# Sums of weight quarters for seven SwiGLU pairs and for the last product: made by GpSimd in the buffers that the products read, instead of ahead and through DRAM

## The chip, the cores and the metric

One core of one Trainium2 chip runs the whole block. The metric is device time in microseconds of one launch; a kernel's time is the median of its runs. The engines are named as the profile names them: PE is TensorE, PEld its weight loads, DVE is VectorE, ACT is ScalarE, POOL is GpSimd and SP is SyncE, which only issues DMAs. A q behind a name is the engine's queue of DMA issues.

## The reference, cut to what matters

Everything is fp32: 512 positions, width 1024, SwiGLU width 2816.

```python
h = rmsnorm(x, norm1_g)
z_glu, z_rx, z_rg, z_ga, z_gb = split(h @ w_in + b_in)     # 2048, 1280, 1280, 1024, 1024
u = z_glu[..., :1024] * sigmoid(z_glu[..., 1024:])
u = silu(layernorm(causal_depthwise_conv(u, 31 taps)))
y_a = u @ conv_w_out + conv_b_out
y_b = (rg_lru(causal_depthwise_conv(z_rx, 4 taps)) * gelu(z_rg)) @ lru_w_out
x = x + (sigmoid(z_ga) * y_a + sigmoid(z_gb) * y_b) @ w_mix_out
h = rmsnorm(x, norm2_g)
x = x + (silu(h @ ffn_w1) * (h @ ffn_w3)) @ ffn_w2          # 1024 -> 2816 -> 1024
out = rmsnorm(x, norm_f_g)
```

The change concerns the weights of the last two lines of products: ffn_w1 and ffn_w3 (1024 x 2816 each) and ffn_w2 (2816 x 1024).

## The kernel before, in words

**A product** of fp32 numbers is made of three fast ones: every operand is split into a high part (a cast to fp32r) and a low part (the number less its high part), and high x high, high x low and low x high are summed in PSUM. For weights the cast is ScalarE's and the subtraction VectorE's or GpSimd's (`split_to`; `sub`, L119, is the one line of nearly all subtractions, and L123 of the casts).

**Weights arrive as chunks.** `wchunk` writes a chunk into a list: its name, its source, its size and the engine that makes the low half. `load_chunk` issues its load into a raw tile of 128x1024 (pool `raws`, RAW = 4 tiles), `emit_chunk` splits it into a tile of high and low halves (pool `hls`, HL = 5), and `weights` emits chunks until the list is AHEAD = 4 past the one that a product asks for. The lists of lru_w_out (tiles lo, 16 chunks of 128x640) and conv_w_out (tiles co, 8 chunks of 128x1024) have their low halves on VectorE, those of w_in (tiles in) on GpSimd.

**Seven products in place of eight.** A product of a 2x2 block matrix with another is made in seven block products. They need, besides the weight's quarters q11, q12, q21 and q22 (b11 and so on as tiles), four sums of them: t3 = q22 - q12, t1 = q12 - q11, t2 = q11 + t3 and t4 = q21 - t2. This scheme serves w_mix_out (class `Quartered`, name m), ffn_w2 (name o, eleven k's with half tiles of 128x512 each), and ten of the eleven SwiGLU pairs (class `Seven`; a pair k is two tiles of 128 columns of ffn_w1 and ffn_w3; the pair k = 0 is done plainly). The pairs 1 to 3 are begun early (BEGUN, BEGUN_LATER), the pairs 4 to 10 run one behind the other: for each, TensorE makes r1 with b11, r2 with b21, r3 with b22, then adds t2, makes r5 with t1, r7 with t3 and adds t4 (`f_product`, matmuls at L1440, tiles fr). Between them VectorE adds the results (L1153) and multiplies the two halves into `ou` and `ov` (L1459), the input of ffn_w2. The last product runs through `Sevenfold` (matmuls at L1204, tiles or): three thirds, each over all eleven k's; the first reads b11, t1 and b21, the second t2, t3 and b22, the last t4.

**Where the sums come from.** For the SwiGLU pairs, a generator (`make_f_sums`) that runs one step per product of the first stages issues the load of a piece of 128x1024 (`piece_load`, pool `wsums`, PIECES = 4 tiles, which also hold the first three tiles of x), its four sums of 128x256 each (`piece_sums`, L119 and L407, on GpSimd), and its store (`piece_store`, L413) into a DRAM tile `f_sums`: 4 pieces for each of ten pairs, 40 in all. For ffn_w2 there are 22 pieces in the same form (tiles fwso, DRAM tiles ot): one in the product of w_mix_out (`mix_end`), the others during the SwiGLU pairs at the places that the table `OUT_PIECES` gives (`out_step`, `due_sums`): GpSimd's queue issues load and store, VectorE makes the sums. The last two pieces of the SwiGLU pairs go the same way (F_LATE). `f_chunks` and `Quartered` then read the sums as chunks, from DRAM. In the program's order VectorE, ScalarE, TensorE and SP have hand-written stretches (`manual_schedule`); elsewhere a scheduler sets the order of instructions on each engine.

Of the kernel before, what the change touches and what calls it, by code (L numbers as in the profile page):

```python
# [32 lines left out]
RAW = 4  # L33
HL = 5
AHEAD = 4
SUMS_BEHIND = 3
# [11 lines left out]
PIECES = 4  # L48


OUT_PIECES = {0: "1", 1: "111", 2: "01", 3: "11", 4: "111", 5: "101", 6: "111", 7: "111", 8: "101", 9: "101", 10: "100"}
# [4 lines left out]
SUMS_AT, SUMS_STEP, SUMS_LAG, STORE_LAG = 3, 3, 2, 2  # L56
STORED_LAG = 3
SUMS_DENSE, SUMS_OWN, SUMS_EACH = 22, 40, (56, 68)


F_LATE, F_AT, OUT_MIX, MIX_LATE_LAG, LATE_LAG = 2, 6, 1, 2, 8
OUT_IN = 0
# [23 lines left out]
def tile_block(ctx, tc, a, out):  # L86
# [5 lines left out]
    wsums = pool("wsums", PIECES)  # L92
# [66 lines left out]
    def load_chunk(i):  # L159
        key, src, kt, cols = chunks[i][:4]  # L160
# [10 lines left out]
    def emit_chunk():  # L171
# [12 lines left out]
        elif where == "hl":  # L184
# [6 lines left out]
            held[key] = (h.rearrange("p (k n) -> p k n", k=kt), l.rearrange("p (k n) -> p k n", k=kt))  # L191
        else:
# [72 lines left out]
    class Quartered:  # L265
        def __init__(self, name, w, kh, lo, parts=(), step=None, on_pool=(), put_off=()):
# [3 lines left out]
            self.step = step or 1  # L270
# [3 lines left out]
            self.all_sums = [dram.tile([P, 4, T], F32, tag=f"{name}t_{k}", name=f"{name}t_{k}") for k in range(kh)]  # L274
            self.sums = {(n, k): self.all_sums[k][:, i, :] for i, n in enumerate(IN_PLACE) if n not in parts for k in range(kh)}
# [17 lines left out]

            for p_ in (("b11", "t1", "b21"), ("t2", "t3", "b22"), ("t4",)):
                p_ = [n for n in p_ if n not in parts]
                for k in range(kh):
                    if len(p_) % 2 and k % 2 == 0:
                        chunk(f"{p_[-1]}_{k}", [(p_[-1], i) for i in (k, k + 1) if i < kh])
                    if len(p_) > 1:
                        chunk(f"{p_[0]}_{k}", [(n, k) for n in p_[:2]])  # L300

# [44 lines left out]
    f_sums = {k: dram.tile([P, 2, 2, 1024], F32, tag=f"fs{k}", name=f"fs{k}") for k in SEVEN}  # L346
# [24 lines left out]

    def f_chunks(k, some=("b2", "t0", "t1")):
# [14 lines left out]
    def o_piece(k, c):  # L387
        four = outq.w.rearrange("p (k h) (e n) -> p h k e n", h=2, e=2)
        cs = slice(256 * c, 256 * c + 256)
        return f"o{k}_{c}", [four[:, h, k, :, cs] for h in range(2)], outq.all_sums[k][:, :, cs]  # L390

    def piece_load(name, halves, queue=nc.sync):
        raw = wsums.tile([P, 1024], F32, tag="wsum", name=f"fws{name}")
# [21 lines left out]
    def make_f_sums():  # L415
# [5 lines left out]
        todo = f_todo[:-F_LATE] + [out_todo.pop(0) for _ in range(OUT_IN)]  # L421
        sums_due, stores_due = [], []
        n, next_at, stored = 0, SUMS_AT, [-9]
        while todo or sums_due or stores_due:
# [5 lines left out]
            if todo and n >= next_at and len(sums_due) + len(stores_due) + (n < stored[0] + STORED_LAG) < PIECES:  # L430
                next_at += SUMS_STEP - (n >= SUMS_DENSE) - (SUMS_EACH[0] <= n < SUMS_EACH[1])
# [17 lines left out]
                if n >= SUMS_EACH[0]:  # L449

                    sums()
                else:
                    sums_due.append((n + SUMS_LAG, sums))
# [9 lines left out]
    for k in range(KF):  # L463
# [4 lines left out]
        elif k in SEVEN:  # L468
            f_both("b11", k)
            f_chunks(k)  # L470
# [8 lines left out]
    outq = Quartered("o", a["ffn_w2"][0].rearrange("(k p) n -> p k n", p=P), NF // 2, vec, step=2, on_pool=("t4_6",))  # L479
# [37 lines left out]
    wide = [wsums.tile([P, 1024], F32, tag="wsum", name=f"x{t}") for t in range(WIDE)]  # L517
# [589 lines left out]
    f_todo = [f_piece(k, i, c) for k in SEVEN for i in range(2) for c in range(2)]  # L1107
    out_todo = [o_piece(k, c) for k in range(KF) for c in range(2)]
# [180 lines left out]
    mix_todo = [out_todo.pop(0) for _ in range(OUT_MIX)]  # L1289
    out_todo[F_AT:F_AT] = f_todo[-F_LATE:]  # L1290
# [6 lines left out]
    def mix_end(second, plus, r1, r2, r7, third):  # L1297
        made = []

        def store():  # L1300
            with tc.issue_after(newest["any"]):
                piece_store(*made.pop(0))

        for name, halves, dest in mix_todo:
            with tc.issue_after(newest["any"]):
                made.append((piece_load(name, halves), dest))
# [16 lines left out]
        with tc.manual_schedule(engines={ET.PE, ET.Activation, ET.DVE}):  # L1323
# [25 lines left out]
            for piece in made:  # L1349
                with tc.issue_after(newest["full"]):  # L1350
                    piece_sums(*piece, pool_e)
# [9 lines left out]
        while made:  # L1361
            store()
# [5 lines left out]
    out_stores, out_n, sums_due = [], [0], []  # L1368
    out_at, out_steps = [None, None], {k: list(v) for k, v in OUT_PIECES.items()}

    def due_sums(now=False):
        for entry in list(sums_due):
            entry[0] -= 1
            if now or entry[0] <= 0:
                sums_due.remove(entry)
                with tc.issue_after(newest["now"]), tc.issue_after(newest["low"]):
                    piece_sums(*entry[1], vec)

    def out_step(k):
        due_sums(True)  # L1380
        stored, begun_ = out_at[1], out_at[0]
        if begun_:
            sums_due.append([SUMS_BEHIND, begun_])
# [343 lines left out]
```

## Time and profile before

| | |
|---|---|
| time, median of 3 runs | 787.7 us (787.61 to 788.7) |
| the profiled execution's span | 785.7 us, 2.0 below that median |
| SwiGLU pairs (tiles f and fr at L1440) | from 449 to 674.7 us |
| last product (tiles or) | from 674.7 to 779.6 us |
| sums of pieces on GpSimd (L119, fws) | 114 instructions, 92.0 us |
| stores and loads of ffn_w2 pieces by GpSimd's queue | 21 stores of 512 KB, 42 loads of 256 KB |
| DMA over the span | 199.04 MB, mean 253 GB/s |
| HBM read, written | 146.30 MB, 38.80 MB |

A row of a group of instructions reads: line, engine, operation, output<-inputs with their shape, how many; then busy us and mean ns of one; then the engine's idle time just ahead of them and what ended it. A row of the chain reads: start, duration, engine, tile, line, count. A row of the windows view reads: stretch and its length, then the engines asked for, each with busy us and the number of instructions, then the granted clock of TensorE, the DMA engines' busy share and GB/s. A row of the timeline reads: start, duration, engine, line, operation, tiles, count. Times are us from the span's start.

### The profile page before, as it was taken

The page shows a single profiled execution, that of the slowest core. Times are in us where ns is not written, and L with a number is a line of the kernel's source. Part 1 is how long each engine was busy: PE and PEld are TensorE (multiplying, and loading weights), DVE is VectorE, ACT ScalarE, POOL GpSimd, SP SyncE. Part 2 cuts the span into 40 slices and gives each one's busy share as a digit, 9 for nine tenths or more (in the row PEclk, how much of TensorE's full clock was granted, in tenths as well). Part 3 has the DMA queues.
Part 4 walks back from the last instruction along what each step waited for, and adds up shares of the span by engine and source line. Part 5 has one row for each costly group of instructions (what it writes and reads, how often), then busy time and mean ns, then how long its engine had stood idle before and what let it go on. Part 6 is the DMA issues. An engine that isn't in the chain of part 4 may idle for free.

```text
span 785.7 us, 12502 instructions
## 1 busy us (share of the span) xinstructions
PE 777.9 (99%) x4327; PEld 680.0 (87%) x4327; DVE 682.8 (87%) x1074; ACT 474.6 (60%) x697; POOL 362.3 (46%) x353
## 2 busy tenths in 40 slices
PE   9999999999999999999999999999999999999996
PEld 8888888888888888888888898999999999888885
DVE  6389998889987988999799869899878888999956
ACT  8543678966785786574235675555554555556844
POOL 4367876789798988654440382122322321000000
PEclk9999999999999999999999999999999999999999
DMA  8556989899899966998978676699998998778652
GB/s 246 164 148 183 290 227 271 239 275 275 249 278 272 274 203 208 331 303 268 306 264 294 189 211 209 192 313 313 348 339 297 325 333 283 226 237 273 196 172 108
DMA packets 188561, 199.04 MB, mean 253 GB/s; under 512 B 15290, under 2 KB 149586, under 8 KB 188498
## 3 DMA queue, kind: packets, MB, share of 16 engines
q1 hardware_dynamic: 178066, 161.80, 68.4%
q0 software_dynamic: 10272, 36.18, 13.2%
q8 instruction: 34, 0.56, 0.3%
q14 instruction: 29, 0.24, 0.1%
q10 hardware_dynamic: 160, 0.27, 0.1%
HBM read 146.30 MB, written 38.80 MB: 236 GB/s over the span
## 4 chain that ended last, share of the span: by engine, by line
PE 98%; DMA 1%; DVE 0%; ACT 0%; SPq 0%; issue 0%
PE z L577 36%; PE fr L1440 25%; PE or L1204 13%; PE yb L577 7%; PE ya L577 6%; PE mxr L1204 5%; PE f L577 3%; PE g L1030 2%; PE fr L1495 1%; DMA x<-in_x_dram 1%; PE tx L638 0%; PE th L622 0%; PE z L695 0%; ACT of L1668 0%; PE orl L1204 0%; DVE n1j L659 0%
## 5 line engine op out<-in xcount | busy, mean ns | idle before, releaser
L830 DVE SCALAR_TENSOR_TENSOR cv<-u,par,cv 128x507 f32<-128x507 f32 (+15 forms) x240 | 162.2, 733 | 4.2 <-ACT cv L826 3.3
L119 POOL TENSOR_TENSOR hl_in<-raw_in,hl_in 128x1024 fp32r<-128x1024 f32 (+1 forms) x52 | 123.8, 2391 | 53.8 <-ACT hl_in L123 44.7
L119 POOL TENSOR_TENSOR fws<-fws 128x256 f32<-128x256 f32 x114 | 92.0, 810 | 44.1 <-DMA fws<-in_ffn_w_dram 38.8
L413 POOL DMA_DIRECT2D ot<-fwso x21 | 15.4, 733 | 132.9 <-DVE fwso L119 125.0
L1440 PE MATMUL fr<-hs_0h,hl_ft 128*128 128x256 f32 x320 | 59.2, 283 | 0.0
L123 ACT CAST hl_ft<-raw_ft 128x1024 fp32r<-128x1024 f32 x40 | 41.7, 1046 | 27.2 <-PE fr L1440 18.5
L119 DVE TENSOR_TENSOR hl_ft<-raw_ft,hl_ft 128x1024 fp32r<-128x1024 f32 x39 | 47.7, 1222 | 10.9 <-ACT hl_ft L123 10.8
L123 ACT CAST hl_in<-raw_in 128x1024 fp32r<-128x1024 f32 x50 | 51.4, 1047 | 1.7 <-PE z L577 1.1
L1440 PEld LDWEIGHTS fr<-hs_0h,hl_ft 128*128 128x128 f32 x320 | 50.6, 192 | 0.0
L1440 PE MATMUL fr<-hs_0l,hl_ft 128*128 128x256 f32 x160 | 45.3, 283 | 0.0
L119 DVE TENSOR_TENSOR hl_fb<-raw_fb,hl_fb 128x1024 fp32r<-128x1024 f32 x29 | 35.5, 1225 | 9.3 <-ACT hl_fb L123 9.3
L123 ACT CAST hl_fb<-raw_fb 128x1024 fp32r<-128x1024 f32 x30 | 31.5, 1049 | 17.9 <-PE fr L1440 8.8
L577 PE MATMUL z<-h10h,hl_in 128*128 128x512 f32 (+1 forms) x108 | 41.1, 382 | 0.0
L577 PE MATMUL z<-h12h,hl_in 128*128 128x512 f32 (+1 forms) x108 | 40.8, 379 | 0.0
L577 PE MATMUL z<-h13h,hl_in 128*128 128x512 f32 (+1 forms) x108 | 40.8, 379 | 0.0
L577 PE MATMUL z<-h14h,hl_in 128*128 128x512 f32 (+1 forms) x108 | 40.8, 379 | 0.0
L577 PE MATMUL z<-h15h,hl_in 128*128 128x512 f32 (+1 forms) x108 | 40.8, 379 | 0.0
L577 PE MATMUL z<-h16h,hl_in 128*128 128x512 f32 (+1 forms) x108 | 40.8, 379 | 0.0
L577 PE MATMUL z<-h11h,hl_in 128*128 128x512 f32 (+1 forms) x108 | 40.8, 379 | 0.0
L577 PE MATMUL z<-h17h,hl_in 128*128 128x512 f32 (+1 forms) x108 | 40.8, 379 | 0.0
L396 POOL DMA_DIRECT2D fwso<-in_ffn_w_dram x42 | 29.9, 716 | 23.7 <-DMA ot<-fwso 21.9
L119 POOL TENSOR_TENSOR hl_ot<-raw_ot,hl_ot 128x1024 fp32r<-128x1024 f32 x1 | 2.4, 2413 | 83.2 <-ACT hl_ot L123 83.2
(949 smaller groups left out, 2629.6 us busy)
## 6 DMA issues: line engine op xcount, KB each, us to landing
raw_in<-in_w_in_dram SPq DMA_DIRECT2D x51, 512.0 KB
fws<-in_ffn_w_dram SPq DMA_DIRECT2D x38, 512.0 KB
raw_ft<-fs SPq DMA_DIRECT2D x34, 512.0 KB
fs<-fws POOLq DMA_DIRECT2D x25, 512.0 KB, 5.2
fwso<-in_ffn_w_dram POOLq DMA_DIRECT2D x42, 256.0 KB, 7.1
ot<-fwso POOLq DMA_DIRECT2D x21, 512.0 KB, 6.0
raw_ob<-in_ffn_w_dram SPq DMA_DIRECT2D x33, 256.0 KB
raw_ot<-ot SPq DMA_DIRECT2D x33, 256.0 KB
```

Source lines behind the costliest of these rows:

```text
L119: return eng.tensor_tensor(out=o, in0=x, in1=y, op=ALU.subtract)
L123: copy(h, full)
L396: queue.dma_start(raw[:, h * n : h * n + n].rearrange("p (e n) -> p e n", n=256), src)
L413: return queue.dma_start(dest, raw.rearrange("p (m n) -> p m n", n=256))
L577: pe.matmul(ps, l, r, start=i == 0, stop=i == n - 1)
L830: vec.scalar_tensor_tensor(out=acc[:, s:], in0=u[c][:, : T - s], scalar=dw(c, s), in1=acc[:, s:], op0=ALU.mult, op1=ALU.add)
L1030: pe.matmul(ps[:HB], head_chunk[0][:ROWS_G, g, h % 2, m, :], ext[h][m][:ROWS_G], start=m == 0, stop=m == 1)
L1204: pe.matmul(banks[i][:, cs], l_[:, ts], r_[:, cs], start=start and n == 0, stop=stop and n == 2, skip_group_check=again)
L1440: pe.matmul(ps[:, HALVES[i]], lw[:, c, :], rx_, start=not (again or i or c or m), stop=bool(i and c == 3 and m == 2), skip_group_check=True,)
L1495: pe.matmul(self.r4[:, HALVES[i]], lw, rx_, start=not (i or c or m), stop=bool(i and c == 3 and m == 2), skip_group_check=True)
```

## The change

1. Only the pairs 1 to 3 keep their stored sums (`STORED`): 12 pieces in place of 40, one every five steps in place of three.
2. The pairs 4 to 10 get `f_fly`: their b11, b12, b21 and b22 are loaded as raw tiles, and GpSimd makes the four sums in place, 128x1024 each. `sums_32` (t3, then t2) is called when b22 has been split, `sums_14` (t1, t4) when t2 has been split; the chunks t2, t1, t3 and t4 are then the same raw tiles, without a load of their own. Low halves stay on VectorE.
3. ffn_w2 gets `Quartered.fly`: raw tiles hold b11 with q12, and t2's q11 with q12, side by side; GpSimd makes t1 (into the q12 half) in the first third, t3 and t2 in the second, keeps a copy of every t2 in a long-lived tile (`ot2r`), and makes t4 from q21, loaded again, and that copy. No DRAM tiles, no `out_step`, no `due_sums`, no `OUT_PIECES`. The low half of ot4_6 goes from GpSimd to VectorE.
4. The pool `wsums` goes; raw tiles become 8 in place of 4, and x's first tiles and the remaining pieces live among them.
5. The low halves of lru_w_out and conv_w_out go from VectorE to GpSimd.

```diff
-RAW = 4
+RAW = 8
...
-PIECES = 4
+PIECES = 3
...
+STORED = BEGUN + BEGUN_LATER
-SUMS_AT, SUMS_STEP, SUMS_LAG, STORE_LAG = 3, 3, 2, 2
+SUMS_AT, SUMS_STEP, SUMS_LAG, STORE_LAG = 3, 5, 2, 2
...
     def load_chunk(i):
-        key, src, kt, cols = chunks[i][:4]
+        key, src, kt, cols, where = chunks[i][:5]
+        if callable(where):
+            loaded_raw[i] = where()
+            return
...
             held[key] = (h.rearrange("p (k n) -> p k n", k=kt), l.rearrange("p (k n) -> p k n", k=kt))
+            if after:
+                after()
...
-            wchunk(f"lo{j}_{hf}", lru_out[:, 5 * hf : 5 * hf + 5, j * P : (j + 1) * P], 5, P, lo=vec)
+            wchunk(f"lo{j}_{hf}", lru_out[:, 5 * hf : 5 * hf + 5, j * P : (j + 1) * P], 5, P)
...
-        wchunk(f"co{j}", conv_out[:, :, j * P : (j + 1) * P], ND, P, lo=vec)
+        wchunk(f"co{j}", conv_out[:, :, j * P : (j + 1) * P], ND, P)
...
+        def fly(self, chunk):
...
+            def one(k):
+
+                def load(raw_t):
+                    nc.sync.dma_start(raw_t, w[:, self.tile(k, 0), :])
+                    sub(pool_e, raw_t[:, T:], raw_t[:, T:], raw_t[:, :T])
...
+            def two(k):
+
+                def load(raw_t):
+                    nc.sync.dma_start(raw_t, w[:, self.tile(k, 0), :])
+                    r22, at = b22[k]
+                    sub(pool_e, raw_t[:, T:], r22[:, at : at + T], raw_t[:, T:])
+                    pool_e.tensor_tensor(out=raw_t[:, :T], in0=raw_t[:, T:], in1=raw_t[:, :T], op=ALU.add)
+                    t2[k] = longt(f"{name}t2r{k}")
+                    pool_e.tensor_copy(t2[k], raw_t[:, :T])
...
+            def four(k, raw_t, at):
+                v = raw_t[:, at : at + T]
+                sub(pool_e, v, v, t2[k])
+
+            for k in range(kh):
+                if k % 2 == 0:
+                    pair("b21", k, lambda *a: None)
+                one(k)
+            for k in range(kh):
+                if k % 2 == 0:
+                    pair("b22", k, keep)
+                two(k)
+            for k in range(0, kh, 2):
+                pair("b21", k, four)
...
+    def f_fly(k):
+
+        q = {}
+
+        def new(n):
+            q[n] = raw_t = raws.tile([P, 1024], F32, tag="raw", name=f"raw_f{n}_{k}")
+            for i, w_ in enumerate((w1, w3)):
+                src = f_quarter(n, k, w_, 0, 4)
+                newest["any"] = nc.sync.dma_start(raw_t[:, i * T : (i + 1) * T].rearrange("p (k n) -> p k n", k=4), src).ins
+            return raw_t
...
+        def sums_32():
+            sub(pool_e, q["b12"], q["b22"], q["b12"])
+            pool_e.tensor_tensor(out=q["b11"], in0=q["b12"], in1=q["b11"], op=ALU.add)
+
+        def sums_14():
+            sub(pool_e, q["b22"], q["b22"], q["b11"])
+            sub(pool_e, q["b21"], q["b21"], q["b11"])
+
+        for n, load, after in (
+            ("b11", first, None), ("b21", lambda: new("b21"), None), ("b22", lambda: new("b22"), sums_32),
+            ("t2", lambda: q["b11"], sums_14), ("t1", lambda: q["b22"], None), ("t3", lambda: q["b12"], None), ("t4", lambda: q["b21"], None),
+        ):
+            wchunk(f"f{n}_{k}", None, 8, P, where=load, lo=vec, after=after)
...
-            f_both("b11", k)
-            f_chunks(k)
+            f_fly(k)
...
-            out_step(k)
```

In the changed program the line of the subtractions is L116 (L119 before), that of the additions L1236 (L1153), that of the halves' product L1498 (L1459); L454 adds in `sums_32`, L327 adds and L329 copies in `two`.

GpSimd's queue during the SwiGLU pairs, before: loads and stores of ffn_w2 pieces (fwso with k and half).

```order
L396 DMA fwso6_1_6328<-in_ffn_w2_dram 128x2x256 x2
L413 DMA ot_5_100<-fwso5_1_6149 512x1x256
L396 DMA fwso7_0_6403<-in_ffn_w2_dram 128x2x256 x2
L413 DMA ot_6_101<-fwso6_0_6256 512x1x256
L396 DMA fwso7_1_6511<-in_ffn_w2_dram 128x2x256 x2
L413 DMA ot_6_101<-fwso6_1_6328 512x1x256
```

The same queue at the same place in the changed program; the number behind a tile's name is its pair k.

```order
L454 TENSOR_TENSOR raw_fb11_6_5652<-raw_fb12_6_5655,raw_fb11_6_5652 128x1024
L116 TENSOR_TENSOR raw_fb12_7_5887<-raw_fb22_7_5956,raw_fb12_7_5887 128x1024
L116 TENSOR_TENSOR raw_fb21_6_5689<-raw_fb21_6_5689,raw_fb11_6_5652 128x1024
L116 TENSOR_TENSOR raw_fb22_6_5724<-raw_fb22_6_5724,raw_fb11_6_5652 128x1024
L454 TENSOR_TENSOR raw_fb11_7_5884<-raw_fb12_7_5887,raw_fb11_7_5884 128x1024
L116 TENSOR_TENSOR raw_fb12_8_6119<-raw_fb22_8_6188,raw_fb12_8_6119 128x1024
L116 TENSOR_TENSOR raw_fb21_7_5921<-raw_fb21_7_5921,raw_fb11_7_5884 128x1024
L116 TENSOR_TENSOR raw_fb22_7_5956<-raw_fb22_7_5956,raw_fb11_7_5884 128x1024
```

Its DMA issues are gone, and four sums of 128x1024 stand there per pair: t3 of the next pair goes ahead of t4 and t1 of this one.

VectorE's queue in the middle of the SwiGLU pairs, before: low halves (hl), sums of ffn_w2 pieces (fwso), additions from PSUM (fr) and products of halves (ov).

```order
L119 TENSOR_TENSOR hl_ft01_7_6338<-raw_ft01_7_6336,hl_ft01_7_6338 128x1024
L407 TENSOR_TENSOR fwso5_1_6149<-fwso5_1_6149 128x256
L1459 TENSOR_TENSOR ov6_6083<-c21_6_6289 128x256
L119 TENSOR_TENSOR fwso5_1_6149<-fwso5_1_6149 128x256
L119 TENSOR_TENSOR hl_ft10_7_6371<-raw_ft10_7_6369,hl_ft10_7_6371 128x1024
L119 TENSOR_TENSOR fwso6_0_6256<-fwso6_0_6256 128x256
L1153 TENSOR_TENSOR c11_7_6365<-fr2_7_6335,c11_7_6365 128x512
L119 TENSOR_TENSOR fwso6_0_6256<-fwso6_0_6256 128x256
```

The same place in the changed program.

```order
L116 TENSOR_TENSOR hl_ft2_7_5993<-raw_fb11_7_5884,hl_ft2_7_5993 128x1024
L1498 TENSOR_TENSOR ov6_5792<-q_6_5917 128x256
L1236 TENSOR_TENSOR c21_6_5988<-fr1_6_5793,c21_6_5988 128x512
L116 TENSOR_TENSOR hl_ft1_7_6027<-raw_fb22_7_5956,hl_ft1_7_6027 128x1024
L1498 TENSOR_TENSOR ov6_5792<-c21_6_5988 128x256
L116 TENSOR_TENSOR hl_ft3_7_6058<-raw_fb12_7_5887,hl_ft3_7_6058 128x1024
L1236 TENSOR_TENSOR c11_7_6054<-fr2_7_6026,c11_7_6054 128x512
```

The sums of pieces are gone from VectorE; the low halves of t2, t1 and t3 now read raw tiles that GpSimd has just summed.

GpSimd's queue in the last product, before, is the end of its program: two stores, one low half and one product of the final norm.

```order
L413 DMA ot_10_105<-fwso10_0_7095 512x1x256
L413 DMA ot_10_105<-fwso10_1_7166 512x1x256
L119 TENSOR_TENSOR hl_ot4_6_8227<-raw_ot4_6_8224,hl_ot4_6_8227 128x1024
L1662 TENSOR_TENSOR of30_8281<-x2b30_7367,gfh_7369 128x256
```

In the changed program its second third holds sums (t3 into the q12 half, t2 into the q11 half of a raw tile) and copies of t2 to a long-lived tile.

```order
L116 TENSOR_TENSOR raw_ot2_3_7451<-raw_ob22_2_7400,raw_ot2_3_7451 128x512
L327 TENSOR_TENSOR raw_ot2_3_7451<-raw_ot2_3_7451 128x512
L329 COPY ot2r0_7359<-raw_ot2_0_7355 128x512
L329 COPY ot2r1_7395<-raw_ot2_1_7391 128x512
L116 TENSOR_TENSOR raw_ot2_4_7522<-raw_ob22_4_7490,raw_ot2_4_7522 128x512
L327 TENSOR_TENSOR raw_ot2_4_7522<-raw_ot2_4_7522 128x512
L329 COPY ot2r2_7446<-raw_ot2_2_7442 128x512
L329 COPY ot2r3_7455<-raw_ot2_3_7451 128x512
```

What VectorE did from pieces ahead of the last product, GpSimd does inside it: 33 sums and 11 copies, with 11 further sums (t1) that stand in part ahead of it.

More of the change, by code (lines that the diff above doesn't have):

```diff
@@ L385, in f_piece @@
         return f"{k}_{i}_{c}", [quarters], f_sums[k][:, i].rearrange("p m (k c n) -> p c m k n", k=2, c=2)[:, c]
[L387 to L390, printed above, removed]
     def piece_load(name, halves, queue=nc.sync):
-        raw = wsums.tile([P, 1024], F32, tag="wsum", name=f"fws{name}")
+        raw = raws.tile([P, 1024], F32, tag="raw", name=f"fws{name}")
         n = 1024 // len(halves)
@@ L415, in make_f_sums @@
     def make_f_sums():
-        todo = f_todo[:-F_LATE] + [out_todo.pop(0) for _ in range(OUT_IN)]
+        todo = list(f_todo)
         sums_due, stores_due = [], []
@@ L516, in tile_block @@
     WIDE = 3
-    wide = [wsums.tile([P, 1024], F32, tag="wsum", name=f"x{t}") for t in range(WIDE)]
+    wide = [raws.tile([P, 1024], F32, tag="raw", name=f"x{t}") for t in range(WIDE)]
     xt = [[w[:, :T], w[:, T:]] for w in wide] + [[longt(f"x{t}{h}") for h in range(2)] for t in range(WIDE, NT)]
@@ L1425, in f_product @@
     def f_product(k, got, ps, x_, w_, again=False, ahead=AHEAD, between=None):
-        both = w_ == "b11" or k in BEGUN + BEGUN_LATER and w_ not in ("t2", "t1")
+        both = w_ == "b11" or k not in STORED or w_ not in ("t2", "t1")
         n, e, first = WHERE.get(w_, (None,) * 3)
@@ L1612, in loads @@
         elif k == 10:
-            assert not out_todo and out_at == [None, None]
             for h in range(2):
```

102 lines of the change are left out of this document (38 added, 64 removed).

## The prediction, made before the changed kernel had run

> **What bounds the kernel now.** I read the busy shares first, then TensorE's own waits, then the chain that ended last.
>
> ```profile
> PE 777.9 (99%) x4327; PEld 680.0 (87%) x4327; DVE 682.8 (87%) x1074; ACT 474.6 (60%) x697; POOL 362.3 (46%) x353
> ...
> PE warm L546 <- DVE ones L538: 1.1, 1, 1.1
> PE tx L638 <- DVE x L678: 0.6, 1, 0.6
> ...
> 332.24 34.03 PE yb L577 x150
> ...
> 366.26 43.52 PE ya L577 x192
> ...
> 499.06 175.68 PE fr L1440 x1464
> 674.74 103.39 PE or L1204 x456
> ```
>
> TensorE (PE) waits twice, 1.7 us together, both before 7 us. From there to 779.6 the chain runs on it without a gap: 1464 products of 256 columns in 175.68 us (0.120 each), 456 of 512 columns in 103.39 (0.227). So nothing that the change removes can shorten the middle; it can only keep TensorE fed or fail to. The question is whether the new route of the sums delivers in time.
>
> Two stages decide. **F** is the seven SwiGLU pairs k = 4 to 10: the pairs 1 to 3 take the first 288 of the 1464 products, so F runs from 499.06 + 288 x 0.120 = 533.6 to 674.7, 141.1 us or 20.16 per pair. **O** is the last product, 674.7 to 779.6. Here are both in the windows view (F above, O below): first all engines (PE, PEld, DVE, ACT, POOL), then VectorE (DVE) and GpSimd (POOL) by line or tile, in this order: L119 (subtractions), tile fwso (sums of w2 pieces, L119 and L407), L407, L1459 (product of two halves), L1153 (additions), tile fr, tile or (both PSUM).
>
> ```profile
> 533.60:674.70 141.10, 141.10 (x1178) 141.10 (x1177) 121.54 (x198) 74.08 (x104) 34.81 (x49) 1.00 0.93 314
> 674.70:779.60 104.90, 104.90 (x469) 86.90 (x467) 93.14 (x152) 63.12 (x99) 3.13 (x2) 1.00 0.64 202
> ...
> 533.60:674.70 141.10, 82.91 (x111) 0.00 (x0) 1.00 0.93 314
> 674.70:779.60 104.90, 71.70 (x103) 2.41 (x1) 1.00 0.64 202
> ...
> 533.60:674.70 141.10, 26.91 (x64) 32.55 (x46) 1.00 0.93 314
> 674.70:779.60 104.90, 1.67 (x4) 0.71 (x1) 1.00 0.64 202
> ...
> 533.60:674.70 141.10, 7.63 (x18) 0.00 (x0) 1.00 0.93 314
> 674.70:779.60 104.90, 0.42 (x1) 0.00 (x0) 1.00 0.64 202
> ...
> 533.60:674.70 141.10, 12.18 (x29) 1.00 0.93 314
> 674.70:779.60 104.90, 0.84 (x2) 1.00 0.64 202
> ...
> 533.60:674.70 141.10, 25.82 (x40) 1.00 0.93 314
> 674.70:779.60 104.90, 16.41 (x29) 1.00 0.64 202
> ...
> 533.60:674.70 141.10, 141.10 (x1177) 140.94 (x1175) 24.93 (x37) 12.35 (x21) 1.00 0.93 314
> 674.70:779.60 104.90, 0.04 (x1) 0.00 (x0) 0.68 (x1) 0.00 (x0) 1.00 0.64 202
> ...
> 674.70:779.60 104.90, 104.35 (x462) 86.05 (x461) 12.64 (x20) 1.00 0.64 202
> ```
>
> The reader is to see that VectorE is 86% and 89% busy in these stages, while GpSimd does no arithmetic in F (its 34.81 us are DMA issues) and next to none in O. The change fills just this gap. Whether a gap on GpSimd is free beside a busy VectorE is the point, and earlier stages, where both work, answer it.
>
> **Two engines, one at a time.** First a group of VectorE whose operands both lie in SBUF (xb, th), and one of the same shape with one operand in PSUM (gr). Then the timeline around 129 us (VectorE, then GpSimd) and around 303 us (the same).
>
> ```profile
> L924 DVE SCALAR_TENSOR_TENSOR xb<-th,xb 128x512 f32<-128x512 f32 x10 | 11.9, 1194 | 0.4 <-DMA th<-tg 0.4
> L924 DVE SCALAR_TENSOR_TENSOR gr<-ea,gr 128x512 f32<-128x512 f32 x10 | 6.9, 687 | 0.1
> ...
> 129.10 2.86 DVE L924 SCALAR_TENSOR_TENSOR xb<-th,xb 128x512 f32<-128x512 f32 x1
> 131.88 0.68 DVE L924 SCALAR_TENSOR_TENSOR gr<-ea,gr 128x512 f32<-128x512 f32 x1
> ...
> 129.00 5.22 POOL L119 TENSOR_TENSOR hl_in<-raw_in,hl_in 128x1024 fp32r<-128x1024 f32 x2 [2.78 <-ACT hl_in L123]
> 134.19 1.29 POOL L119 TENSOR_TENSOR xb5l<-xb,xb5h 128x512 fp32r<-128x512 f32 x1
> ...
> 302.84 3.67 DVE L119 TENSOR_TENSOR hl_lo<-raw_lo,hl_lo 128x640 fp32r<-128x640 f32 x1
> 306.44 0.68 DVE L928 TENSOR_TENSOR z<-xb,z 128x512 f32<-128x512 f32 x1
> ...
> 303.01 1.43 POOL L407 TENSOR_TENSOR fws<-fws 128x256 f32<-128x256 f32 x2
> 304.40 1.43 POOL L119 TENSOR_TENSOR fws<-fws 128x256 f32<-128x256 f32 x2
> ```
>
> The VectorE instruction with both operands in SBUF that starts 0.1 us behind a GpSimd subtraction lasts 2.86 us; with one operand in PSUM it lasts 0.68. At 302.84 such an instruction stands through four GpSimd sums and ends 0.69 us after the last (305.83). The two queues do not share: one waits. The pair at 129.00 also gives the price of a turn. VectorE ends at 131.96, GpSimd's second subtraction at 134.22; its pace alone would be 2.37 (estimate: half of 5.22 less the 0.45 that it stood), so VectorE's turn cost GpSimd 0.45 us where VectorE's own pace is 0.60 (0.68 less the 0.08 by which its rows overlap: 129.10 + 2.86 against 131.88). About 0.15 us per turn is given back.
>
> The Trainium skill, page SBUF — State Buffer, section Who interferes with whom, says that a VectorE instruction with two SBUF inputs contends with GpSimd's reads, and that who starts first keeps the port pair for the whole instruction. By that rule nothing would be given back, and the sums below would be 5.0 and 7.5 us longer. The rows say 0.15 per turn, so the sums go by them; on which instructions collide they agree.
>
> **The change, part by part.** GpSimd's prices, with the nearest rows:
>
> ```profile
> L119 POOL TENSOR_TENSOR hl_in<-raw_in,hl_in 128x1024 fp32r<-128x1024 f32 x50 | 121.2, 2435 | 47.0 <-ACT hl_in L123 44.7 <-DMA raw_gate<-in_lru_wx_dram 0.9 <-DMA ext<-xb2l 0.8
> L119 POOL TENSOR_TENSOR hl_in<-raw_in,hl_in 128x512 fp32r<-128x512 f32 x2 | 2.6, 1291 | 6.7 <-ACT hl_in L133 6.6
> L133 POOL CAST hl_in<-raw_in 128x512 fp32r<-128x512 f32 x1 | 0.6, 616 | 0.0
> ```
>
> *Added.* In F four sums of 128x1024 per pair, 28 x 2.37 = 66.4 us, and by its order GpSimd also makes about five of the first w2 sums there (5 x 1.29 = 6.5): 72.9. In O the other 39 sums of 128x512 (44 in all) and 11 copies: 39 x 1.29 + 11 x 0.62 = 57.1. The copy has no row of its own; the cast is nearest, and 0 or 1.29 would move O by -7 or +7.
>
> *Removed.* VectorE's w2 sums: in F 64 of 26.91 us, in O 4 of 1.67. VectorE keeps, with both operands in SBUF: in F (82.91 - 26.91 + 7.63) + 12.18 + (25.82 - 24.93) = 76.7 us in 97 instructions; in O (71.70 - 1.67 + 0.42) + 0.84 + (16.41 - 12.64 - 0.68) = 74.4 in 110. Less 0.08 each: 68.9 and 65.6. With an operand in PSUM: F 24.93 in 37 (paced 22.0), O 13.3 in 21 (11.6).
>
> *The sum.* One at a time, F needs 72.9 + 68.9 less 33 turns x 0.15 = 136.8 us of 141.1, and O 57.1 + 65.6 - 7.5 = 115.2 of 104.9. VectorE's queue is in order, so its 22.0 and 11.6 us on PSUM are free only where GpSimd happens to hold the port. GpSimd is on for half of both stages. If all of it hides, F gains no time and loses none (a lead is bounded by the buffers) and O is 10.3 late; if half does, F is at 147.8 (+6.7) and O at 121.0 (+16.1). I take the middle, F +3.4 and O +13.2: **+16.6**. The ends: all hidden and turns given back as well as around 351.5 us (next rows) give +4; nothing hidden gives F +17.7 and O +21.9, +40.
>
> ```profile
> 351.73 1.23 DVE L119 TENSOR_TENSOR un3l<-u,un3h 128x512 fp32r<-128x512 f32 x1
> ...
> 351.54 2.01 POOL L119 TENSOR_TENSOR fws<-fws 128x256 f32<-128x256 f32 x2 [2.83 <-DMA fws<-in_ffn_w_dram]
> ```
>
> There four GpSimd sums and four VectorE instructions run from 351.54 to 356.45, 4.91 us, where their own paces add to about 5.5: a factor of 0.89, which would bring O to 0.89 x 122.7 = 109.2, +4.
>
> *Moved or at no cost.* The low halves of lru_w_out and conv_w_out go to GpSimd: two of 128x640 per product (1.58 us each by the rows above, an estimate between 512 and 1024) beside 30 products of 0.227 = 6.8 us, and 2.4 beside 5.44; chunks are made four ahead, so both hide; without that cover the first costs 3.2 us once. The sums of seven pairs go from the first 400 us, with their stores and loads: TensorE waits for no DMA there, so 0. RAW 8 for 4 + 4 buffers, x in those buffers: same transfers, 0. **The new waits:** ScalarE's cast of t2 and t1 now stands behind GpSimd, and behind it in ScalarE's queue stand the copy of the next pair's first product and the activations; from the second sum to TensorE's need lie about 9 us in F at the prices alone. GpSimd's copies in O wait for a tile that TensorE frees (the second for the end of k = 5's second product, 22.9 us into O, the seventh for the first third's end at 44.9); 19 us of GpSimd's work follows that one and has until 98, so it costs nothing by itself.
>
> Against its own time: 785.7 + 16.6 = 802.3 for the span; the median is 787.7, 2.0 more, so 804.3. I say **804**.
>
> **The rivals.** *The sums hide* (the other side, 787.7): GpSimd may work as far ahead as eight raw buffers allow, and if its work and VectorE's fit side by side more than the rows show, TensorE never waits. It decides at O's 104.9 us against 109.2 in the best packing seen. TensorE's 1.7 us of waits before 7 us are out of reach, so faster by over 0.2% (1.6 us, about what a measurement here can tell from none) would need a shorter tail, for which no row speaks. *A loop through the buffers* in F: a pair's raw tiles are freed by the low part of t4 two pairs before, then come load, three sums and a cast: 5 + 3 x 3.3 + 1, with about 4 for t4's own cast and turn, 20 us against 20.16. Were it 22, each of seven pairs would lose 2, and with O's 13 the time would be 787.7 + 14 + 13 = 815. For it: each sum stands behind a subtraction of 1.2. Against it: the load of 0.5 MB may be quicker. *VectorE starves* as at 302.84, with none of its PSUM work hidden: +40, 827.
>
> **How the numbers follow.** Forecast (port time in O, a little in F) 0.55, loop 0.17, starving 0.15: all slower. Hidden 0.13, of which 0.09 within 0.2%, 0.03 faster, 0.01 slower. So slower 0.88, same 0.09, faster 0.03. The range goes from 790 (best packing, 2 us below its 792) to 825, leaving out the hidden case and the end of starving.
>
> **What would show it.** In the changed profile PE should stand idle in O, above all in its second third, with DVE or ACT named before it; VectorE's subtractions of 128x1024 should average well over 1.22 us in F and O, and its additions from PSUM stay at 0.68. If PE has no gap in O, the sums of the port are wrong. If most of the loss lies in F, the loop was the cause. If the lru_w_out or conv_w_out stages open gaps, the cover there was misjudged.

## The result, and the profile after

The changed kernel takes **821.87 us** (median of 4 runs, 820.61 to 822.41) where the kernel before takes 787.71: a ratio of 1.043, 95% interval 1.0415 to 1.0445. It is 34.2 us slower; the forecast was 16.6 slower.

First the busy line of the page after, then what TensorE waited for, then four rows of the chain that ended last (the products of lru_w_out and conv_w_out, and F).

```profile
PE 788.0 (96%) x4327; PEld 683.4 (83%) x4327; DVE 722.9 (88%) x959; ACT 470.9 (57%) x697; POOL 443.7 (54%) x265
...
PE or L1287 <- DVE hl_ot L116: 13.2, 4, 5.5
PE or L1287 <- DVE hl_ob L116: 8.2, 3, 6.6
PE or L1287 <- DVE x2b L1236: 2.1, 3, 1.3
...
312.00 20.43 PE yb L661 x90
332.89 34.03 PE yb L661 x150
366.92 43.52 PE ya L661 x192
...
499.72 127.67 PE fr L1480 x1064
```

The products yb and ya last what they lasted before, and F has no wait: apart from 1.1 us at the start, which the kernel before has too, every wait of more than 0.6 us stands in O, most of it behind low halves that VectorE made late. By TensorE's first and last rows O starts at 675.23 (674.58 before), and its end moves from 779.62 to 813.88. So all but 0.65 us of the loss lies there. Here are O's thirds in the windows view (PE, PEld, DVE, ACT, POOL), of before and then of after; a third begins with the first matmul on its own operands, the last with the end of those on oeb.

```profile
674.58:719.49 44.91, 44.91 (x201) 37.17 (x199) 44.31 (x81) 26.98 (x40) 0.71 (x1) 1.00 0.78 246
719.49:764.53 45.04, 45.04 (x200) 37.32 (x199) 35.86 (x47) 28.22 (x39) 0.18 (x1) 1.00 0.65 203
764.53:779.62 15.09, 15.09 (x72) 12.53 (x71) 13.09 (x27) 8.07 (x21) 2.23 (x1) 1.00 0.19 71
```

```profile
675.23:732.09 56.86, 48.02 (x201) 38.07 (x199) 54.56 (x81) 29.32 (x45) 41.18 (x13) 0.94 0.55 180
732.09:797.99 65.90, 50.92 (x199) 39.43 (x197) 65.69 (x47) 27.03 (x36) 61.95 (x38) 0.92 0.33 116
797.99:813.88 15.89, 15.64 (x72) 12.64 (x72) 14.53 (x30) 8.06 (x21) 0.00 (x0) 1.00 0.18 67
```

The first third is 11.9 us longer, the second 20.9, the last 0.8. Of these 33.6 us TensorE stood 24.1; its matmuls were busy for the other 9.5 (114.58 us in place of 105.04). The rows of before point to the reason: VectorE was busy for 44.31 of 44.91 us in the first third and 35.86 of 45.04 in the second, where the prediction had read one mean of 89% over O. After the change GpSimd makes all its sums of O in these two thirds (five already ahead of them) and none in the last.

How the two engines meet there shows in the groups of after and in its timeline (VectorE from 691 us, then GpSimd).

```profile
L116 DVE TENSOR_TENSOR hl_fb<-raw_fb,hl_fb 128x1024 fp32r<-128x1024 f32 x29 | 50.6, 1747 | 5.6 <-ACT hl_fb L120 4.6
L116 DVE TENSOR_TENSOR hl_ft<-raw_fb,hl_ft 128x1024 fp32r<-128x1024 f32 x28 | 44.3, 1580 | 0.4 <-ACT hl_ft L120 0.4
L1236 DVE TENSOR_TENSOR x2b<-or,x2b 128x512 f32<-128x512 f32 x19 | 12.2, 679 | 1.2 <-PE or L1287 1.2
L116 POOL TENSOR_TENSOR raw_ob<-raw_ob 128x512 f32<-128x512 f32 x11 | 35.6, 3248 | 28.7 <-DMA raw_ob<-in_ffn_w_dram 24.9
...
691.06 0.41 DVE L116 TENSOR_TENSOR os1p<-os,os1p 128x256 fp32r<-128x256 f32 x1
...
707.32 0.42 DVE L116 TENSOR_TENSOR oe<-ou,ov 128x256 f32<-128x256 f32 x1
710.01 1.23 DVE L116 TENSOR_TENSOR hl_ob<-raw_ob,hl_ob 128x1024 fp32r<-128x1024 f32 x1 [2.26 <-ACT hl_ob L120]
...
691.13 21.26 POOL L116 TENSOR_TENSOR raw_ob<-raw_ob 128x512 f32<-128x512 f32 x3 [5.49 <-DMA raw_ob<-in_ffn_w_dram]
```

VectorE's subtractions with two operands in SBUF grew from 1.22 to 1.75 and 1.58 us; its additions from PSUM stayed at 0.68. The last row begins at 691.13: the first of its three sums t1, which take 1.28 us at the shortest, lasts 17.77 us and ends just after VectorE first runs dry, at 707.74. In between VectorE worked through 32 instructions at their own pace (0.41 us for 128x256), one right behind the other, and GpSimd did not get in once.

### The profile page after: what moved, and what is told of

The parts are those of the page before. It is cut to its first block, busy times and chain, and to the rows that moved or that the text cites. A ratio compares the mean times of both kernels' runs of the same rounds, so it can differ in the third digit from the quotient of the medians.

```text
span 820.1 us, 12207 instructions
## 1 busy us (share of the span) xinstructions
PE 788.0 (96%) x4327; PEld 683.4 (83%) x4327; DVE 722.9 (88%) x959; ACT 470.9 (57%) x697; POOL 443.7 (54%) x265
## 4 chain that ended last, share of the span: by engine, by line
PE 79%; DVE 12%; issue 3%; DMA 2%; POOL 2%; ACT 0%; SPq 0%; DVEq 0%; POOLq 0%; ACTq 0%
PE z L661 34%; PE fr L1480 18%; PE yb L661 7%; PE ya L661 5%; PE mxr L1287 5%; PE or L1287 4%; PE f L661 3%; POOL raw_ob L116 2%; PE g L1114 2%; DVE hl_ob L116 2%; DVE hl_ot L116 1%; DMA raw_ob<-in_ffn_w_dram 1%; DVE hl_ft L116 1%; PE fr L1534 1%; DVE hl_fb L116 1%
## 5 line engine op out<-in xcount | busy, mean ns | idle before, releaser
L116 POOL TENSOR_TENSOR hl_in<-raw_in,hl_in 128x1024 fp32r<-128x1024 f32 (+1 forms) x52 | 122.7, 2369 | 95.1 <-ACT hl_in L120 74.3
L116 POOL TENSOR_TENSOR raw_fb<-raw_fb,raw_fb 128x1024 f32<-128x1024 f32 x21 | 58.8, 2821 | 62.4 <-DMA raw_fb<-in_ffn_w_dram 51.0
L116 DVE TENSOR_TENSOR hl_fb<-raw_fb,hl_fb 128x1024 fp32r<-128x1024 f32 x29 | 50.6, 1747 | 5.6 <-ACT hl_fb L120 4.6
L116 POOL TENSOR_TENSOR raw_ob<-raw_ob 128x512 f32<-128x512 f32 x11 | 35.6, 3248 | 28.7 <-DMA raw_ob<-in_ffn_w_dram 24.9
L116 DVE TENSOR_TENSOR hl_ft<-raw_fb,hl_ft 128x1024 fp32r<-128x1024 f32 x28 | 44.3, 1580 | 0.4 <-ACT hl_ft L120 0.4
L116 POOL TENSOR_TENSOR hl_lo<-raw_lo,hl_lo 128x640 fp32r<-128x640 f32 x16 | 26.4, 1655 | 27.6 <-ACT hl_lo L120 27.6
L454 POOL TENSOR_TENSOR raw_fb<-raw_fb,raw_fb 128x1024 f32<-128x1024 f32 x7 | 18.8, 2688 | 37.9 <-issue 30.1
L120 ACT CAST hl_ft<-raw_fb 128x1024 fp32r<-128x1024 f32 x28 | 28.6, 1046 | 17.5 <-POOL raw_fb L116 9.6
```

The costliest lines, as they stand in the source:

```text
L116: return eng.tensor_tensor(out=o, in0=x, in1=y, op=ALU.subtract)
L120: copy(h, full)
L454: pool_e.tensor_tensor(out=q["b11"], in0=q["b12"], in1=q["b11"], op=ALU.add)
```

## The experiments

Theory A is the prediction's: the two engines share one way into SBUF, and O had no room for GpSimd's work on it. Rival B is a loop of buffers, loads and waits that the new route brings, whoever makes the sums; C to E stand in the expectations where they are tested.

**Is it O's sums, or the route? (o_none, f_none)** Both leave sums out: o_none those of O with their copies, f_none those of F.

```diff
-                    sub(pool_e, raw_t[:, T:], raw_t[:, T:], raw_t[:, :T])
...
-                    pool_e.tensor_copy(t2[k], raw_t[:, :T])
...
-            sub(pool_e, q["b12"], q["b22"], q["b12"])    # f_none: these of F in place of those above
-            pool_e.tensor_tensor(out=q["b11"], in0=q["b12"], in1=q["b11"], op=ALU.add)
```

> The changed kernel without the 44 sums and 11 copies of the last product (O): the raw quarters are split and multiplied in place of the sums, so the product is not the reference's; loads, buffers, splits and matmuls stay. Theory A (GpSimd and VectorE take turns at one way into SBUF, and O's first two thirds have room for VectorE's work alone): 787 to 792 us, PE without gaps in O. Theory B (the loop of buffers, loads and small new waits costs it, whoever makes the sums): over 805 us. Theory C (F's sums leave VectorE late at the start of O): between, about 800 us.

Measured: 787.45 us beside 787.34, ratio 1.0003 (0.9994 to 1.0012).

> The changed kernel without the 28 sums of the seven SwiGLU pairs (F): the raw quarters are multiplied in their place, so the pairs are not the reference's; all else, with O's sums, stays. Theory A: 817 to 823 us, since F lost nothing and O keeps its port work. Theory C (F's sums leave VectorE late at the start of O): 800 to 810 us.

Measured: 818.34, ratio 1.0396 (1.038 to 1.0411). The route without O's sums costs nothing that can be measured, and F's 28 sums are in that kernel. F's sums cost some 3 us, in O's first third (54.1 us in place of 56.9); C is a small part at most.

**Is it dependence, or mere company? (add_sums, add_sets)** The kernel before, with GpSimd work in O on a tile that nothing else reads.

```diff
+                pool_e.tensor_copy(dm[:, :1], dep[:, :1].bitcast(F32))
+                for _ in range(sums):
+                    sub(pool_e, dm[:, :T], dm[:, T:], dm[:, T:])    # add_sets: pool_e.memset(dm, 0.0)
```

> The kernel before, with GpSimd work added to O that nothing waits for: per k of the first third one subtraction of 128x512 on a tile of its own, per k of the second third three and one copy, each group behind a copy of one column that waits for a low part made in that k. About 42 sums and 10 copies, 60 us at their own pace. No chunk, buffer or wait of the product changes. Theory A: 808 to 822 us (60 us of GpSimd and 72 of VectorE in 90). Theory B: 788 us, for nothing depends on the added work.

Measured: 812.07, ratio 1.0317 (1.03 to 1.0334).

> As add_sums, but each added sum is a memset of 128x1024 and each copy a memset of 128x512: GpSimd writes and reads nothing but the one column per k. Theory A with reads as what collides: 787 to 790 us. If any busy GpSimd slows VectorE, writes too: as add_sums in proportion to its busy time.

Measured: 787.36, ratio 1.0000 (0.999 to 1.0009). Thirds of add_sums, then the first two of add_sets; behind each, a copy of one column by GpSimd from the first third, and for add_sums TensorE's two longest waits.

```profile
674.62:719.52 44.90, 44.90 (x200) 37.18 (x199) 44.06 (x79) 26.85 (x40) 37.55 (x8) 1.00 0.75 242
719.52:777.54 58.02, 49.57 (x199) 38.87 (x197) 55.91 (x47) 28.18 (x38) 54.84 (x45) 0.94 0.52 162
777.54:804.21 26.67, 17.37 (x72) 13.83 (x72) 15.28 (x29) 8.17 (x21) 16.97 (x17) 0.81 0.11 41
...
PE or L1204 <- POOL hl_ot L119: 8.9, 1, 8.9
PE or L1204 <- DVE hl_ot L119: 8.4, 3, 4.0
...
L1232 POOL COPY dm<-ous3l x1: 30378/30378/30378, 682.3 to 682.3; 128x1 f32<-128x1 f32 x1
```

```profile
674.35:719.25 44.90, 44.90 (x200) 37.18 (x199) 44.30 (x81) 26.98 (x40) 34.79 (x24) 1.00 0.75 243
719.25:764.30 45.05, 45.05 (x200) 37.34 (x199) 35.87 (x47) 28.23 (x39) 33.17 (x45) 1.00 0.64 205
...
L1232 POOL COPY dm<-ous4l x1: 19256/19256/19256, 685.2 to 685.2; 128x1 f32<-128x1 f32 x1
```

The added work costs 24.7 us when it reads SBUF and nothing when it only writes, with 33 us of GpSimd busy in the second third and VectorE at 35.87 as before. It isn't quite work that nothing waits for, as the expectation has it: GpSimd's own low half of ot4_6 stands behind it in its queue. So the 24.7 us have two parts. The second third is 13.0 us longer, and there TensorE waits for VectorE (8.4); that is A's. The last is 11.6 longer, and there it waits 8.9 us for GpSimd's low half, which comes late because the added work, shut out and slowed before, ends only at 793. The 13.0 us put B out for O: apart from 2.3 us that ScalarE waits at 715 us behind an added copy, nothing in the second third waits for the added work. In the first third GpSimd's copy stood 30.4 us and VectorE lost nothing: shut out, GpSimd did no harm until someone needed its result. The Trainium skill, SBUF — State Buffer, Who interferes with whom, says that a VectorE instruction with two SBUF inputs contends with a GpSimd instruction that reads SBUF and not with one that only writes it; these two runs agree.

**How much of the work, and whose? (copy_act, no_t4, no_t1, o_dve, all_dve)**

```diff
-                    pool_e.tensor_copy(t2[k], raw_t[:, :T])
+                    act.copy(t2[k], raw_t[:, :T])
...
-                sub(pool_e, v, v, t2[k])    # left out in no_t4, with the copies
+                sub(vec, v, v, t2[k])    # o_dve, with every other sum of O
```

> The changed kernel with the 11 copies of t2 in O made by ScalarE in place of GpSimd; the result is the same. Theory A (one way into SBUF for the two engines): 6.2 us of GpSimd's work leave the second third, of which 0.88 counted there: 815 to 818 us. Theory D (what costs is GpSimd being shut out by a stream of VectorE, so that sums come late, and not the amount of work): 820 to 822 us, or more where ScalarE's queue waits for the copies.

Measured: 815.34, ratio 1.0356 (1.034 to 1.0371). The total is as A said, the split is not: O's thirds take 59.9, 49.5 and 23.1 us, where the changed kernel's take 56.9, 65.9 and 15.9. Seven of GpSimd's sums (10.05 us) now run in the last third.

> The changed kernel without the 11 sums t4 and the 11 copies of t2 in O: q21 is multiplied in place of t4, so the last product isn't the reference's. Theory A: 20 us of GpSimd's work leave the second third, of which 0.88 counts: 802 to 807 us. Theory D: the sums that TensorE waits for in the first two thirds are still there: 815 us or more.

Measured: 808.39, ratio 1.0262 (1.0247 to 1.0278). Less gain than A gave, more than D: the second third fell to 53.8 us, not 48.

> The changed kernel without the 11 sums t1 of O: the raw q12 is multiplied in place of t1, so the last product isn't the reference's. Theory A counted by thirds: the first third, in which VectorE alone has 42.7 of 44.9 us, goes from 56.9 back to 45 to 49 us, the second stays at 66: 810 to 814 us. Theory D (late sums through GpSimd being shut out): the same first third, but t3 and t2 then come earlier too, and the second third gains as well: under 806 us.

Measured: 813.05, ratio 1.0326 (1.031 to 1.0341). The total is as A said, the split again is not: the first third fell only to 52.3, the second to 63.0. That t3 and t2 move up into the place that t1 left would account for it, but was not tested by itself.

> The changed kernel with the 44 sums of O on VectorE (0.60 us each in place of 1.25 on GpSimd) and the 11 copies on ScalarE; the result is the same. Nothing of GpSimd is left in O but one product at the end. Theory A: VectorE's own queue is longer by 5 us in the first third and by up to 20 in the second, where it has about 10 free: 796 to 806 us. Theory E (sums inside the product are late whoever makes them, since load, sum, cast and subtraction stand in a row): 815 us or more.

Measured: 805.84, ratio 1.0229 (1.0212 to 1.0247). Its thirds:

```profile
675.64:725.33 49.69, 46.69 (x200) 36.51 (x198) 49.69 (x90) 26.09 (x41) 0.00 (x0) 1.00 0.59 203
725.33:775.31 49.98, 46.94 (x198) 36.63 (x198) 49.93 (x70) 35.13 (x52) 0.00 (x0) 1.00 0.50 163
775.31:798.40 23.09, 17.61 (x72) 13.51 (x72) 21.98 (x41) 9.99 (x23) 0.00 (x0) 0.93 0.12 46
```

VectorE is busy throughout with no GpSimd beside it: now its own work is the bound, 18 us over, and E, which gave 815 us or more, is out. O has no room for the sums on either engine. With the copies on ScalarE in both, the sums cost 28 us on GpSimd (copy_act) and 18 on VectorE.

> As o_dve, and F's 28 sums on VectorE too (1.14 us each). VectorE then has 91 + 32 = 123 us of 141 in F, without a collision. Theory A: as o_dve within 3 us. If F's sums on VectorE delay its low halves: slower than o_dve by 5 us and more, with gaps of PE in F.

Measured: 805.19, ratio 1.0221 (1.0205 to 1.0236): F takes its sums on either engine.

**How near to the edge is F? (f_extra, f_sets)** Both start from o_none.

```diff
+        for cs in (slice(0, T), slice(T, 2 * T)):
+            sub(pool_e, spare[0], x[:, cs], y[:, cs])    # f_sets: a copy of one column of x, seven memsets of spare[0]
```

> The kernel without O's sums (787.5 us), with 28 more subtractions of 128x512 on GpSimd in F, two ahead of t3 and two ahead of t1 and t4 of each pair, into a tile that nothing reads; the last product isn't the reference's. GpSimd then has 99 us of work in F's 141, VectorE 69 with two operands in SBUF. Theory A: F had 141 less 132.6 less the turns, some 13 us free, and 31 to 35 come: F is 18 to 22 us longer, 803 to 812 us. If F's sums cost nothing because GpSimd and VectorE do not collide there: 787 to 790 us.

Measured: 820.13, ratio 1.0415 (1.0399 to 1.043): more than A gave.

> As f_extra (O's sums left out, so the last product isn't the reference's), but the 28 added subtractions of F are 98 memsets of 128x512 (14 per pair, 0.53 us each, 7.4 us per pair) and 14 copies of one column that put them in place: GpSimd is as long busy, but writes only. If F's extra time came from the port (theory A): 787 to 790 us. If it came from the loop of one pair (GpSimd's sums, ScalarE's casts behind them, VectorE's low half of the next b11, then the next t2), whose length in f_extra was 25.3 us against TensorE's 20.16 per pair: a loop of 22 to 25 us, so 800 to 821 us.

Measured: 813.69, ratio 1.0331 (1.0316 to 1.0347). GpSimd around one pair in after, f_extra and f_sets (L454, L458 and L460 are the sum t2 of the next pair, two rows apart by one pair), with TensorE's wait of the last two and, for f_extra, VectorE's low half of the next b11:

```profile
607.46 2.48 POOL L454 TENSOR_TENSOR raw_fb<-raw_fb,raw_fb 128x1024 f32<-128x1024 f32 x1 [7.67 <-issue]
611.10 8.29 POOL L116 TENSOR_TENSOR raw_fb<-raw_fb,raw_fb 128x1024 f32<-128x1024 f32 x3 [1.16 <-DMA raw_fb<-in_ffn_w_dram]
627.07 2.40 POOL L454 TENSOR_TENSOR raw_fb<-raw_fb,raw_fb 128x1024 f32<-128x1024 f32 x1 [7.68 <-issue]
```

```profile
PE fr L1485 <- ACT c L1522: 20.9, 7, 4.8
...
604.44 2.41 POOL L458 TENSOR_TENSOR raw_fb<-raw_fb,raw_fb 128x1024 f32<-128x1024 f32 x1 [7.08 <-issue]
606.93 7.50 POOL L116 TENSOR_TENSOR spare<-raw_fb,raw_fb 128x512 f32<-128x512 f32 x4
614.50 8.15 POOL L116 TENSOR_TENSOR raw_fb<-raw_fb,raw_fb 128x1024 f32<-128x1024 f32 x3
629.74 2.41 POOL L458 TENSOR_TENSOR raw_fb<-raw_fb,raw_fb 128x1024 f32<-128x1024 f32 x1 [7.08 <-issue]
...
628.39 1.22 DVE L116 TENSOR_TENSOR hl_fb<-raw_fb,hl_fb 128x1024 fp32r<-128x1024 f32 x1
```

```profile
PE fr L1487 <- ACT c L1524: 16.9, 5, 5.7
...
601.70 3.15 POOL L460 TENSOR_TENSOR raw_fb<-raw_fb,raw_fb 128x1024 f32<-128x1024 f32 x1
...
625.65 0.50 POOL L436 COPY spare<-raw_fb 128x1 f32<-128x1 f32 x1 [6.41 <-DMA raw_fb<-in_ffn_w_dram]
...
626.70 2.41 POOL L460 TENSOR_TENSOR raw_fb<-raw_fb,raw_fb 128x1024 f32<-128x1024 f32 x1
```

A alone does not account for F: added work that only writes costs 26 us too. In f_extra the trace shows a loop of 25.3 us through three engines. GpSimd's last sum of the round shown ends at 622.65; ScalarE has waited 8.37 us for it and casts it from 622.69; VectorE then makes four low halves in its queue's order, the last of them that of the next b11, which ends at 629.61; t2, which overwrites b11, starts 0.13 us behind it, in this round and in five others. TensorE waits for ScalarE's copy of r1, which stands in ScalarE's queue behind that cast. Turns at SBUF lengthen the loop: at GpSimd's own paces (4 x 1.29 + 4 x 2.37 = 14.6 us in place of 18.1) a round would take 21.9, by estimate, still 1.7 over TensorE's 20.16.

f_sets doesn't repeat that loop. Ahead of t2 its queue has the added copy of one column, and in four rounds GpSimd stands there for a load, 26.2 us in all. So it shows that F can be lengthened without added collisions, not what f_extra would cost without them. In the changed kernel TensorE never waits in F, so its rounds of 19.5 to 20.2 us go with TensorE's pace and do not measure the loop's own length; in three of four of them 1.0 to 1.7 us is slack ahead of a load.

**Is the pairs' part free in a kernel that is whole? (o_early, o_early2, o_early3)** F as in the change; the sums of O made ahead, as 22 pieces.

```diff
-    f_todo = [f_piece(k, i, c) for k in STORED for i in range(2) for c in range(2)]
+    f_todo = [f_piece(k, i, c) for k in STORED for i in range(2) for c in range(2)] + [o_piece(k, c) for k in range(KF) for c in range(2)]
...
-    outq = Quartered("o", a["ffn_w2"][0].rearrange("(k p) n -> p k n", p=P), NF // 2, vec, step=2, fly=True)
+    outq = Quartered("o", a["ffn_w2"][0].rearrange("(k p) n -> p k n", p=P), NF // 2, vec, step=2)
```

> The changed kernel with its seven pairs as they are (28 sums on GpSimd beside the products), but the sums of the last product taken out of O: 22 pieces as in the kernel before, loaded, summed by GpSimd and stored to DRAM in the first 410 us, in the places that the pairs' 28 pieces have left free; O reads them as the kernel before does. The result is the same. Theory A: 787 to 790 us, no gap of PE in F or O, since GpSimd does nothing in O and the early stages had these sums before. Theory E (buffers and loads of the new route): over 795 us.

Measured: 806.79, ratio 1.0241 (1.0224 to 1.0258). O takes 44.9, 45.0 and 15.1 us, but it starts 19.7 us later than before. VectorE, GpSimd and TensorE around 410 us:

```profile
405.13 8.44 DVE L117 TENSOR_TENSOR mxe<-mxu,mxv 128x256 f32<-128x256 f32 x1
...
407.68 2.87 POOL L117 TENSOR_TENSOR fwso<-fwso 128x256 f32<-128x256 f32 x4
410.45 1.46 POOL L502 TENSOR_TENSOR fwso<-fwso 128x256 f32<-128x256 f32 x2
411.84 1.44 POOL L117 TENSOR_TENSOR fwso<-fwso 128x256 f32<-128x256 f32 x2
...
423.12 0.79 PE L1293 MATMUL mxr<-hl_mxb,mxus0h 128*128 128x512 f32 x1 [8.28 <-DVE hl_mxb L117]
```

The other way round: a subtraction of 0.42 us on VectorE stands for 8.44 behind a stream of ten of GpSimd's sums, and TensorE later stands for 8.28.

```diff
-            wchunk(f"lo{j}_{hf}", lru_out[:, 5 * hf : 5 * hf + 5, j * P : (j + 1) * P], 5, P)
+            wchunk(f"lo{j}_{hf}", lru_out[:, 5 * hf : 5 * hf + 5, j * P : (j + 1) * P], 5, P, lo=vec)
```

> As o_early, with the low halves of lru_w_out and conv_w_out on VectorE again and the 34 pieces issued as densely as the 38 of the kernel before, so that none is left to be made in one stream behind conv_w_out's product. The result is the same. If o_early's 19 us came from GpSimd's last stream of sums (VectorE stood 8.44 and 5.85 us behind it at 405 and 415 us) and from the low halves beside it: 787 to 790 us. If the new route of the pairs costs them: 800 us or more still.

Measured: 805.25, ratio 1.0222 (1.0205 to 1.0239). So this expectation missed as the last one did: the stream is gone, and the 18 us come back as VectorE's wait for weights of w_mix_out, whose loads stand in SP's queue until stores of pieces have landed (12.1 us by the trace). TensorE stands for 10.2 us at the end of the longest of these waits. In VectorE's list of waits:

```profile
DVE mxws L117 <- DMA mxws<-in_w_mix_out_dram: 18.8, 3, 12.9
```

```diff
-RAW = 8
+RAW = 4
...
+    wsums = pool("wsums", PIECES)
```

> As o_early2, but the pieces, x and half of the pairs' raw tiles (b12 and b22) lie in a pool of four tiles of their own and the chunks in another of four, as in the kernel before, and the pieces are as dense as there. The result is the same. In o_early2 VectorE waited 18.8 us for weights of w_mix_out that were loaded behind pieces in the pool of eight. If that sharing was the cause of its 18 us: 787 to 790 us, with no gap of PE. If the sums of the pieces beside the early stages are: 800 us or more.

Measured: **788.82**, ratio 1.0017 (1.0007 to 1.0026), TensorE with no wait over 1.1 us. Its busy line and DMA line:

```profile
PE 778.5 (99%) x4327; PEld 680.0 (86%) x4327; DVE 692.0 (88%) x983; ACT 472.3 (60%) x697; POOL 369.4 (47%) x289
...
DMA packets 188943, 158.65 MB, mean 202 GB/s; under 512 B 14394, under 2 KB 159954, under 8 KB 188882
```

This run changed the pools, the place of b12 and b22 and the spacing of the pieces together, so it does not say which of them counted. The pairs' part of the change, with a pool of its own for the pieces, is thus slower than the kernel before by 0.17% (0.07 to 0.26) and moves 40 MB less (199.04 to 158.65). No version beats the kernel before: TensorE is busy for 777.9 of its 785.7 us.

## Why the prediction was right in the cause and wrong in the size

- **What bounds the kernel, and where it breaks.** Right: TensorE had no slack, the loss is O's and above all its second third's, DVE is named before its gaps, and additions from PSUM kept 0.68 us.
- **Two engines, one at a time.** Shown for O by the second third of add_sums against that of add_sets.
- **The failing step is the sum of O**: "O 57.1 + 65.6 - 7.5 = 115.2 us ... of 104.9". Two things in it were wrong. First, the time it was set against. GpSimd's 39 sums and 11 copies had to be done before the last third, so they had 89.95 us, not 104.9 (where seven of them were not, in copy_act, that third took 23.1 us in place of 15.1); and VectorE's share is 44.31 of 44.91 in the first third. The prediction knew the thirds and used them for the copies only. Second, "less 0.08 each" took 8.8 us of overlap out of rows of the windows view that already count overlapping time once. Taken by thirds after the result, with the prediction's own prices: the first has 44.31 - 1.96 (its additions from PSUM) + 13 x 1.29 - 13 x 0.15 = 57.2, measured 56.86; the second 35.86 - 5.37 + 26 x 1.29 + 11 x 0.62 - 37 x 0.15 = 65.3, measured 65.90. (13 and 37 are GpSimd's instructions that start there; 1.96 and 5.37 are VectorE's rows on tile or in those windows of before.) With 15.1 for the last that is 137.6 against 138.65: +32.6 of O's 33.6. The count leaves in the four w2 sums that VectorE lost (1.67 us), since 81 instructions of VectorE stand in the first third before and after. It is a count made to fit one run, and it fits others less well: no_t4's second third is 48 by it and 53.8 measured, and copy_act's thirds went another way. How much of the loss is time at SBUF and how much is sums that come late, and with them their cast and low half, is not separated.

```profile
674.58:719.49 44.91, 1.96 (x3) 1.00 0.78 246
719.49:764.53 45.04, 5.37 (x10) 1.00 0.65 203
```

- **The price of a turn** (0.15 us) and **PSUM work beside GpSimd** fit that count with all of the PSUM work hidden, not half. The middle between all hidden and none, which the prediction took, was 2.9 us too dear in O; the deadline outweighed it. By the rule of the Trainium skill that the prediction weighs (SBUF — State Buffer, Who interferes with whom: the port pair is held for the whole instruction, so nothing is given back) the two thirds would come to 130.0; measured are 122.76, and the row decides.
- **F +3.4**: wrong. F lost nothing. What bounds it once GpSimd has more to do is a **loop**, but not the rival's at "20 us against 20.16": that one goes through a freed buffer and a load, and in f_extra GpSimd waits for no load. The rival's price was right in kind: a loop 5.1 us longer than TensorE's pair came out as 32 us over seven pairs.
- **lru_w_out and conv_w_out at no cost**, copies that wait in O at no cost by themselves: right for the first (20.43, 34.03, 43.52 us as before); without the copies on GpSimd the kernel gained 6.5 us (copy_act), near the 6.8 that the sum had for them, though the thirds moved by +3.0, -16.4 and +7.2.
- **Starving** at 827 was nearest in time, but not by its mechanism: VectorE's PSUM work was hidden.

## What to carry to other kernels

Ask of moved work not only whether an engine is idle but by when it must be done: take the busy share of each stretch up to that point, not of the stage. Beside a VectorE that subtracted SBUF from SBUF, GpSimd's arithmetic that reads SBUF was not free, while work that only wrote was (add_sets). An engine's idle time can be part of a loop through other engines: GpSimd's 7 us per pair in F were, and nothing shows in the time until the slack is used up. Follow what ends the idle time before filling it.

## What the runs showed of the hardware

- VectorE and GpSimd did not always take turns at SBUF. An engine that arrived while the other ran without a gap could stand through many instructions: GpSimd through 32 of VectorE's in after (17.77 us), 60 in add_sums (30.38) and 38 in add_sets (19.26, for a copy of one column), VectorE through ten of GpSimd's in o_early (8.44). Elsewhere they took turns (711 to 722 us in after). What decides between the two wasn't found.
- In some stretches where TensorE had gaps its granted clock was lower (0.94 and 0.92 in O's first two thirds of after, 0.81 in the last third of add_sums), in others not (1.00 in o_dve's first two thirds, with 3.0 us of gaps in each). The same 201 matmuls of the first third were busy for 48.02 us in after in place of 44.91; in o_dve, at 1.00, 200 were busy for 46.69, so the clock alone does not account for it. Whether longer matmuls lengthened the run was not separated; in after's second third VectorE was busy for 65.69 of 65.90 us.
